# One weight tile moved off the bias table's buffers, and a load order changed, in a fused transformer layer

## The chip, the cores and the metric

The kernel runs on one core of one Trainium2 chip. The metric is the device time of one launch in microseconds; the median of three runs before the change is 919.48 us (918.82 to 919.53).

## The reference

One layer of a model with 512 tokens of width 1024, all in float32: a first gated feed-forward block (hidden width 2816), a mixer with two kinds of attention, a second feed-forward block, and a final norm. Cut to what matters here:

```python
def swiglu(x, w_gate, w_up, w_down):
    return (jax.nn.silu(x @ w_gate) * (x @ w_up)) @ w_down

x = x + 0.5 * swiglu(rmsnorm(x, ffn1_norm), ffn1_w_gate, ffn1_w_up, ffn1_w_down)
x = x + token_mixer(rmsnorm(x, mix_norm), w_in, w_out, ..., rel_bias)
x = x + 0.5 * swiglu(rmsnorm(x, ffn2_norm), ffn2_w_gate, ffn2_w_up, ffn2_w_down)
return rmsnorm(x, final_norm)
```

`rel_bias` (32 buckets by 16 heads) is spread into one row of biases per head before the mixer's attention starts. The change touches the end of the first feed-forward block, where `... @ w_down` is formed and the bias rows are made in passing.

## The kernel before

**Precision.** Every float32 matrix is split into a high part (a cast, on ACT) and a low part (the rest, a subtraction on DVE). A product is three matmuls into the same PSUM bank (lines 174, 175 and 176 of a helper): high by high, high by low, low by high. Where a weight block is the moving operand, the first and third matmul read its high part and the second (line 175) its low part. So each 128x512 weight block costs a load, a cast on ACT (line 469), a subtraction on DVE (line 473) and matmuls on PE.

**The down projection of the first block.** The 22 hidden tiles of 128 fall into 2 "plain" ones (`PLAIN`, tiles 0 and 1) and two groups of ten. Each group is five pairs of tiles, and is computed with seven block products instead of eight (Strassen's scheme): `a11`, `a22`, `s2`, `a12`, `s1`, `s3`, `s4`, in that order, each over the five pairs (index 0 to 4). One step (`STEP`, 1410 in the planner's units of about a nanosecond) is one pair of one product. In the second group the product of the plain tiles for the first half of the tokens, 24 matmuls into the banks `pc`, stands between `s1` and `s3`; its other half follows after the group.

**What feeds them.** The left upper weight blocks for `a11` are loaded into tiles `ra` (`raa` in the traces; pairs 0 and 1, and 2 and 3, share one 128x1024 buffer each, pair 4 has one of its own), those for `a22` into `re` (`place` puts pair 0 into the tile `rbc_n`, pairs 1 and 2 into two `ob` tiles `rea`, pair 3 into `sq`, pair 4 into a slot, also named `rea`). Sums of blocks (`sCa` for `s1`, `sBa` for `s3`) are loaded by SP and added to by a second, accumulating DMA from POOL. The blocks of `a12` are `rba`, `rbc_n` and `sq` again.

**What sets the order.** On all engines the order of instructions in this stage is the program's own. A planner puts events with times on a heap and emits them in order of time; each engine then runs its part in that order and waits only on semaphores. The table `TURNED["a"]` holds the numbers. Its entry `ahead` says for each product how many steps before the start of its *group* the load of each pair is emitted (`block_events`, with `block_load` doing the load). SP issues nearly all plain loads, and a load whose buffer is not free yet holds up those behind it.

**The plain weights.** At the group's end the weights of the two plain tiles come as four 128x512 blocks: output columns 0 to 511 (`dh` 0) and 512 to 1023 (`dh` 1), two blocks each. `plain_load` loads them, `plain_high` casts the high part (line 1254), `plain_low` subtracts for the low part (line 1257), each between the casts and subtractions of the products `s2` and `a12`. For `dh` 0 high and low part lie in the first two thirds of the tile `wx`, a buffer of 128x3072 with the tag `tx`. For `dh` 1 they are two tiles `wxh` and `wxl` of 128x1280 with the tag `pr1`. That tag has two buffers, which its tiles take in turn: a new tile waits until everything that used the tile two before it is done.

**The bias table.** `bias_load` takes a tile `ac` of the same tag `pr1` for the table (16x640). ACT and DVE change it in place (`bias_rows`, lines 1224 and 1228), and POOL stores it to DRAM as `bias_rows` (line 1229). The attention reads it back from there in strips (line 1234).

Of the kernel before, what the change touches and what calls it, by code (L numbers as in the profile page):

```python
# [15 lines left out]
F32R = mybir.dt.float32r  # L16
# [5 lines left out]
P = 128  # L22
# [54 lines left out]
    "b": {"plain": 2, "pairs": ((2, 4, 6, 8, 10), (12, 14, 16, 18, 20)),  # L77
          "sets": {2: (2, 3, 24, 25, 20, 21, 26), 4: (28, 29, 30, 31, 32, 33, 34), 6: (35, 36, 37, 38, 39, 40, 41),
# [23 lines left out]
HS = S // 2  # L102
# [11 lines left out]
def tile_macaron(ctx: ExitStack, tc, xs, xT, wf, wgu1, wst1, wdg1, wqk, wvw, wv, wo, wgu2, wst2,  # L114
# [7 lines left out]
    tp = ctx.enter_context(tc.tile_pool(name="tp", bufs=2))  # L122
# [1130 lines left out]
    def cast(o, a):  # L1253
        A.copy(o, a)
# [4 lines left out]
    closing, early_w, early_raw = {}, {}, {}  # L1259
# [9 lines left out]
    def plain_high(dh, k):  # L1269
        if k == 0:  # L1270
            if dh == 0:
                tx = tp.tile([P, 12 * HS], F32R, tag="tx", name="wx", bufs=1)
                closing[dh] = tx[:, :1024], tx[:, 1024:2048]
            else:
                closing[dh] = [tp.tile([P, 5 * HS], F32R, tag="pr1", name=f"wx{n}")[:, :1024] for n in "hl"]
        cast(closing[dh][0][:, k * 512:(k + 1) * 512], closing["raw", dh][k])

    def plain_low(dh, k):
# [66 lines left out]
    def close(at, begin, end, ah, al):  # L1345
        closing["tiles"] = ah, al
        gap = begin + 25 * STEP
        last = gap + TILES_STEP + 5 * STEP
        todo = [(begin + 2 * STEP, 1.5, plain_load, 0), (begin + 3 * STEP, 1.5, plain_load, 1),
                (begin + 5 * STEP, 1.5, early_load, 0, 0), (begin + 7 * STEP, 1.5, early_load, 0, 1),  # L1350
                (begin + 20.5 * STEP, 5, A.activation, root[:], eps[:], AF.Sqrt),
                (last - 1.8 * STEP, 1.6, early_load, 1, 0),
                (last + 0.4 * STEP, 1.6, early_load, 1, 1)]
        for n, t in enumerate((10, 11.5, 13, 14.5)):
            todo.append((begin + t * STEP, 4.5, plain_high, n // 2, n % 2))
            todo.append((begin + (t + 1) * STEP, 2.6, plain_low, n // 2, n % 2))
        for t, part in ((-4.2, (0, 0, 0, 512)), (-3.4, (0, 0, 512, 512)), (-2.6, (0, 1, 0, 512)), (-1.8, (0, 1, 512, 512))):
            todo.append((gap + t * STEP, 4.6, early_high, *part))
            todo.append((gap + (t + 0.9) * STEP, 2.7, early_low, *part))
        for tt in range(2):  # L1360
            t = gap + (tt + 1) * TILES_STEP // 2
            for dh in range(2):
                todo.append((t - (1 - dh) * TILES_STEP // 4 + 100, 0, plain_add, dh, tt))
            todo.append((t + 0.6 * STEP, 4, squared, 0, tt))
        for tt in range(2):
            todo += [(last + (0.6 + 0.5 * tt) * STEP, 4, squared, 1, tt),
                     (last + (1.3 + 0.8 * tt) * STEP, 0, mean, tt),
                     (last + (1.6 + 0.8 * tt) * STEP, 0, root_part, tt)]
            todo += [(last + (2.0 + 0.8 * tt) * STEP, 3, scaled, dh, tt) for dh in range(2)]
        for time, rank, f, *a in todo:  # L1370
            at(time, rank, f, *a)
        return plain_mm
# [869 lines left out]
```

## Time and profile before

| | |
|---|---|
| median of 3 runs | 919.48 us (918.82 to 919.53) |
| profiled execution, its own time | 921.12 us |
| its span, first to last instruction | 919.3 us |
| PE / DVE / ACT / POOL busy | 908.2 / 733.0 / 558.3 / 98.8 us |
| mean granted TensorE clock | 0.997 |
| first block's second group: `a11` starts | 280.32 us into the span |
| plain product starts | 320.12 us into the span |

Busy times are sums over one execution. PE is busy nearly throughout, so what can be gained is where it isn't, or where its matmuls follow each other more slowly than elsewhere. Times in the timeline are counted from the start of the span. A figure in square brackets is the time for which the engine sat idle before the instruction, with what ended the wait by the profile's inference. Where a wait is for several things, the profile names the one that it takes to be last; if the named one was done long before, it was another.

### The profile page before, as it was taken

How to read it: one execution, taken by the hardware profiler on the slowest of the kernel's cores; microseconds unless marked ns; L12 is line 12 of the kernel's file. 1: busy time of each engine (PE TensorE's matmuls, PEld its weight loads, DVE VectorE, ACT ScalarE, POOL GpSimd, SP SyncE). 2: the span in 40 equal slices, each digit the busy share in tenths (PEclk: the TensorE clock that was granted, in tenths of full speed). 3: DMA queues.
4: the chain of work that ended last, by engine and by line, in shares of the span. 5: the costliest groups of instructions: out<-in, count | busy, mean ns of one | idle time of the engine just before them, and what ended most of it. 6: DMA issues, size and time to landing. Idle time of an engine off the chain costs nothing.

```text
span 919.3 us, 16048 instructions
## 1 busy us (share of the span) xinstructions
PE 908.2 (99%) x5778; PEld 819.0 (89%) x5778; DVE 733.0 (80%) x1531; ACT 558.3 (61%) x1185; POOL 98.8 (11%) x123
## 2 busy tenths in 40 slices
PE   9999999999999899999999999999999999999997
PEld 7888998899998689888988878989999889999885
DVE  7798998878888687757866536798888887888886
ACT  7445765465667446655776676657665536666664
POOL 0001102121211000000000000010211213112200
PEclk9999999999999999999999999999999999999999
DMA  7454878587878513324434204355878859778722
GB/s 260 123 152 133 228 218 229 115 206 213 201 189 251 160 47 98 92 93 115 138 107 123 69 24 138 92 149 134 207 171 250 192 134 251 178 188 202 219 80 91
DMA packets 67247, 143.88 MB, mean 157 GB/s; under 512 B 7712, under 2 KB 8224, under 8 KB 67168
## 3 DMA queue, kind: packets, MB, share of 16 engines
q1 hardware_dynamic: 51312, 113.81, 38.1%
q0 software_dynamic: 15856, 29.06, 19.6%
q8 instruction: 45, 0.74, 0.3%
q14 instruction: 34, 0.28, 0.1%
HBM read 137.55 MB, written 2.14 MB: 152 GB/s over the span
## 4 chain that ended last, share of the span: by engine, by line
PE 91%; DVE 4%; DMA 3%; ACT 1%; issue 1%; SPq 0%; DVEq 0%; ACTq 0%
PE pt L175 6%; PE pt L174 6%; PE pt L176 6%; PE pq L174 2%; PE pwo L174 2%; PE pq L175 2%; PE pq L176 2%; PE pk L174 2%; PE pk L176 2%; PE pk L175 2%; PE pwo L175 2%; PE pwo L176 2%; PE pua L174 2%; PE pua L176 2%; PE pua L175 2%; PE pga L174 1%
## 5 line engine op out<-in xcount | busy, mean ns | idle before, releaser
L1735 ACT ACTIVATE pr<-pr,mx 128x128 f32<-128x128 f32 (+3 forms) x64 | 36.0, 563 | 36.7 <-DVE mx L1732 36.4
L569 DVE SCALAR_TENSOR_TENSOR x<-pt,x 128x512 f32<-128x512 f32 x52 | 34.4, 686 | 19.4 <-PE pt L176 14.0
L1732 DVE CUSTOM_DVE_ANT_0 pr<-sc,strip 128x128 f32<-128x128 f32 (+3 forms) x64 | 30.5, 489 | 23.1 <-PE sc L1730 22.6
L405 POOL DMA_DIRECT2D s1bg<-wst_dram x10 | 8.7, 868 | 333.4 <-DVE fin L1391 233.3
L473 DVE TENSOR_TENSOR w<-s2b,w 128x512 fp32r<-128x512 f32 x38 | 26.1, 686 | 7.0 <-ACT w L469 7.0
L469 ACT CAST w<-raa 128x512 fp32r<-128x512 f32 x31 | 19.0, 621 | 18.7 <-DVE raa L432 8.0
L469 ACT CAST w<-s2b 128x512 fp32r<-128x512 f32 x38 | 23.6, 620 | 8.4 <-DVE s2b L437 8.4
L174 PE MATMUL pwo<-w,mh 128*128 128x512 f32 x64 | 25.9, 404 | 0.0
L175 PE MATMUL pwo<-w,mh 128*128 128x512 f32 x64 | 25.0, 391 | 0.0
L176 PE MATMUL pwo<-w,ml 128*128 128x512 f32 x64 | 25.0, 391 | 0.0
L473 DVE TENSOR_TENSOR w<-s2a,w 128x512 fp32r<-128x512 f32 x30 | 20.5, 685 | 4.4 <-ACT w L469 4.3
L1523 DVE TENSOR_TENSOR w<-raw_qk,w 128x512 fp32r<-128x512 f32 x24 | 16.4, 687 | 7.9 <-ACT w L1519 7.8
L469 ACT CAST w<-s2a 128x512 fp32r<-128x512 f32 x30 | 18.6, 621 | 6.4 <-DVE s2a L437 6.0
L175 PE MATMUL pxgb<-ttb,w 128*128 128x256 f32 x80 | 22.5, 281 | 0.0
L469 ACT CAST w<-rab 128x512 fp32r<-128x512 f32 x26 | 15.7, 621 | 9.6 <-PE pt L176 5.6
L473 DVE TENSOR_TENSOR w<-raa,w 128x512 fp32r<-128x512 f32 x31 | 20.7, 680 | 0.0
L405 POOL DMA_DIRECT2D s1ag<-wst_dram x8 | 7.1, 888 | 125.0 <-DVE ala L275 40.1
L1729 PE MATMUL sc<-k,q 128*128 128x128 f32 (+3 forms) x64 | 20.5, 322 | 0.0
L1730 PE MATMUL sc<-l,q 128*128 128x128 f32 (+3 forms) x64 | 20.2, 322 | 0.0
L175 PE MATMUL pxub<-ttb,w 128*128 128x256 f32 x72 | 20.2, 281 | 0.0
L175 PE MATMUL pwga<-xl,w 128*128 128x256 f32 x64 | 18.0, 281 | 0.0
L176 PE MATMUL pwga<-xh,w 128*128 128x256 f32 x64 | 18.0, 281 | 0.0
(1101 smaller groups left out, 3921.9 us busy)
## 6 DMA issues: line engine op xcount, KB each, us to landing
raw_qk<-wqk_dram SPq DMA_DIRECT2D x12, 512.0 KB, 3.5
raw0bg<-wst_dram SPq DMA_DIRECT2D x10, 512.0 KB, 4.8
raw0bu<-wst_dram SPq DMA_DIRECT2D x9, 512.0 KB, 5.8
raw_gua<-wgu_dram SPq DMA_DIRECT2D x8, 512.0 KB, 3.6
raw0ag<-wst_dram SPq DMA_DIRECT2D x8, 512.0 KB, 5.0
strip<-bias_rows SPq DMA_DIRECT2D x16, 256.0 KB, 3.5
raw_wo<-wo_dram SPq DMA_DIRECT2D x8, 512.0 KB, 3.4
raw0au<-wst_dram SPq DMA_DIRECT2D x7, 512.0 KB, 6.7
```

The source lines that it names most:

```text
L174: T.matmul(po, wh, mh, start=first, stop=False, skip_group_check=on)
L175: T.matmul(po, wh, ml, start=False, stop=False, skip_group_check=on)
L176: T.matmul(po, wl, mh, start=False, stop=last, skip_group_check=on)
L405: nc.gpsimd.dma_start(t[:], b, accum_op=ALU.add)
L469: A.copy(made[t][0], source(t))
L473: V.tensor_tensor(l, source(t), h.bitcast(F32), op=ALU.subtract)
L569: V.scalar_tensor_tensor(o, a, f, b, op0=ALU.mult, op1=op1)
L1523: V.tensor_tensor(l[:, c:c + 512], raw[:, c:c + 512], h[:, c:c + 512].bitcast(F32), op=ALU.subtract)
L1729: T.matmul(ps[:, :w], qs[:, qi], ks[:, :w], start=True, stop=False)
L1730: T.matmul(ps[:, :w], qs[:, qi], ls[:, :w], start=False, stop=True)
L1732: V.tensor_tensor_reduce(out=pi, in0=ps[:, :w], in1=st["b"][m][:, w - 1::-1], op0=ALU.add, op1=ALU.min, scale=1.0, scalar=3.0e38, accum_ou ...
L1735: A.activation(pi, pi, AF.Exp, scale=-1.0, bias=st["mx"][:, m, i:i + 1], accum_out=st["ls"][:, m, i:i + 1])
```

## The change

Two edits, no other:

```diff
-                    "a11": ((11, 10, 5.9, 5.8, 4.6), (11, 10, 5.9, 5.8, 6)),
-                    "a22": ((6.5, 6.3, 3.8, 0.5, 5), (6.5, 6.3, 3.8, 0.5, 4)),
+                    "a11": ((11, 10, 5.9, 5.8, 4.6), (11, 10, 5.9, 5.8, 4.8)),
+                    "a22": ((4.4, 4.2, 3.2, 0.5, 1.5),) * 2,
...
             if dh == 0:
-                tx = tp.tile([P, 12 * HS], F32R, tag="tx", name="wx", bufs=1)
+                tx = closing["tx"] = tp.tile([P, 12 * HS], F32R, tag="tx", name="wx", bufs=1)
                 closing[dh] = tx[:, :1024], tx[:, 1024:2048]
             else:
-                closing[dh] = [tp.tile([P, 5 * HS], F32R, tag="pr1", name=f"wx{n}")[:, :1024] for n in "hl"]
+                closing[dh] = (closing["tx"][:, 2048:],
+                               tp.tile([P, 5 * HS], F32R, tag="pr1", name="wxl")[:, :1024])
```

**The tiles.** The high part of the plain weights with `dh` 1 goes into the last third of `wx`, which was unused. Only the low part `wxl` still takes a `pr1` buffer. Before, `wxh` took the buffer that follows the bias table's and `wxl` the bias table's own; now `wxl` takes the one that `wxh` had. No instruction moves by this. What changes is what an instruction waits for. DVE at the two low parts of `dh` 1, before, with the semaphores that each row waits for (`DMASW` are those of the DMAs from POOL, `DMAHW` those of the DMAs from SP):

```order
L473 TENSOR_TENSOR w<-rba_3308,w 128x512 [waits DMAHW0_49,Activation_49]
L1257 TENSOR_TENSOR wxl<-deadh_3274,wxh 128x512 [waits DMAHW3_49,DMASW3_49,Activation_49]
L569 SCALAR_TENSOR_TENSOR x_100<-pt_3221,x_100 128x512 [waits Activation_49]
L569 SCALAR_TENSOR_TENSOR x_101<-pt_3222,x_101 128x512 [waits Activation_49]
L473 TENSOR_TENSOR w<-sq,w 128x512 [waits DMAHW3_49,PE_49]
L1257 TENSOR_TENSOR wxl<-deadl_3275,wxh 128x512 [waits DMAHW4_49]
```

And after:

```order
L473 TENSOR_TENSOR w<-rba_3308,w 128x512 [waits DMAHW0_49,Activation_49]
L1257 TENSOR_TENSOR wxl<-deadh_3274,wx 128x512 [waits DMAHW3_49,Activation_49]
L569 SCALAR_TENSOR_TENSOR x_100<-pt_3221,x_100 128x512 [waits Activation_49]
L569 SCALAR_TENSOR_TENSOR x_101<-pt_3222,x_101 128x512 [waits Activation_49]
L473 TENSOR_TENSOR w<-sq,w 128x512 [waits DMAHW3_49,PE_49]
L1257 TENSOR_TENSOR wxl<-deadl_3275,wx 128x512 [waits DMAHW4_49]
```

The rows are the same in the same order; the wait on `DMASW3` at the first row of line 1257 is gone.

**The loads.** On SP, the loads for `a22` move behind those for `a11` in both groups of the first block. SP at the start of the second group, before (`raa` are blocks of `a11`; `rbc_n`, `rea` and `sq` of `a22`; `sBa` of `s3`):

```order
L516 DMA rbc_n_401<-wdg_dram 128x512
L516 DMA rea_3111<-wdg_dram 128x512
L505 DMA raa_3115<-wdg_dram 128x512
L510 DMA raa_3131<-wdg_dram 128x512 x2
L516 DMA rea_3150<-wdg_dram 128x512
L516 DMA rea_3166<-wdg_dram 128x512
L516 DMA sq<-wdg_dram 128x512
L523 DMA sBa_3248<-wdg_dram 128x512
```

And after:

```order
L510 DMA raa_3126<-wdg_dram 128x512 x2
L505 DMA raa_3144<-wdg_dram 128x512
L516 DMA rbc_n_401<-wdg_dram 128x512
L516 DMA rea_3147<-wdg_dram 128x512
L516 DMA rea_3164<-wdg_dram 128x512
L516 DMA rea_3195<-wdg_dram 128x512
L516 DMA sq<-wdg_dram 128x512
L523 DMA sBa_3248<-wdg_dram 128x512
```

The three later loads of `a11` have passed the first two of `a22`. In the first group the same happens around the loads of residual tiles `x` that stand between. PE, DVE, ACT and POOL keep their order in the whole program.

## The prediction

> **What bounds the kernel now.** I read the page first, for which engine the time hangs on:
>
> ```profile
> span 919.3 us, 16048 instructions
> PE 908.2 (99%) x5778; PEld 819.0 (89%) x5778; DVE 733.0 (80%) x1531; ACT 558.3 (61%) x1185; POOL 98.8 (11%) x123
> PE 91%; DVE 4%; DMA 3%; ACT 1%; issue 1%; SPq 0%; DVEq 0%; ACTq 0%
> ```
>
> PE is busy for 908.2 of 919.3 us, and the chain that ended last runs on PE for 91%. The change neither removes nor adds a matmul, so it can only act where PE stands still or runs slowly. The list of waits of PE alone says where it stands still after its warm-up:
>
> ```profile
> PE pt L175 <- DVE w L473: 3.3, 2, 3.1
> PE pt L1820 <- ACT ptx L1822: 0.2, 1, 0.2
> ```
>
> One gap of 3.1 us, a small one behind it in the same two lines (0.2), and nothing else longer than 0.2. PE's timeline at the long one, in the product `a12` of the second group:
>
> ```profile
> 301.52 0.39 PE L174 MATMUL pt<-w,h1a 128*128 128x512 f32 x1
> ...
> 305.60 0.39 PE L174 MATMUL pt<-w,h1a 128*128 128x512 f32 x1
> 309.05 0.50 PE L175 MATMUL pt<-w,h1a 128*128 128x512 f32 x1 [3.06 <-DVE w L473]
> 309.38 0.39 PE L176 MATMUL pt<-w,h2a 128*128 128x512 f32 x1
> ...
> 310.31 0.59 PE L174 MATMUL pt<-w,xl 128*128 128x512 f32 x1
> ...
> 313.69 0.43 PE L176 MATMUL pt<-w,h4a 128*128 128x512 f32 x1
> ```
>
> 18 matmuls start between 301.52 and 305.60, one each 0.227 us: the undisturbed pace. The next start comes 3.45 us later, at a matmul of line 175, which reads a low part. From 310.31 to 313.69 there are 8 starts, one each 0.42 us. The window over them shows why:
>
> ```profile
> 310.30:313.70 3.40, 3.40 (x10) 2.60 (x9) 2.93 (x6) 3.12 (x6) 0.00 (x0) 0.51 0.50 120
> ```
>
> The third column from the end is PE's granted clock: 0.51 for 3.4 us, about the ratio of 0.227 to 0.42. PE's idleness is paid a second time.
>
> What PE waited for is DVE's low part of a weight. DVE's own timeline:
>
> ```profile
> 299.84 1.27 DVE L473 TENSOR_TENSOR w<-rba,w 128x512 fp32r<-128x512 f32 x2
> 306.50 0.69 DVE L1257 TENSOR_TENSOR wxl<-deadh,wxh 128x512 fp32r<-128x512 f32 x1 [5.39 <-ACT w L469]
> 307.12 1.28 DVE L569 SCALAR_TENSOR_TENSOR x<-pt,x 128x512 f32<-128x512 f32 x2
> 308.31 0.68 DVE L473 TENSOR_TENSOR w<-sq,w 128x512 fp32r<-128x512 f32 x1
> ```
>
> DVE stood 5.39 us before `wxl`, with the low part that PE needed (`w<-sq`) three instructions behind it. The profile's releaser is a guess. Asked by tile, the store of the bias table says more:
>
> ```profile
> L1229 POOL DMA_DIRECT2D bias_rows<-ac x1: 762/762/762, 301.4 to 301.4; - x1
> DMA to landing us min/median/max: 5.0/5.0/5.0
> ```
>
> 301.4 + 5.0 = 306.4, and `wxl` starts at 306.50. `wxl` lies in the buffer from which that store reads, and waited for it to land.
>
> **Edit one: the tiles.** It takes that wait away: `wxl` goes where `wxh` was, and nothing on ACT had to wait for that buffer. The new place of `wxh` is the unused third of a tile already in use here. So DVE can start `wxl` at 301.1 (299.84 + 1.27). What is late next? Behind `wxl` stand two additions to `x`, which wait for ACT, and then `w<-sq`. By tile and on ACT:
>
> ```profile
> L513 SPq DMA_DIRECT2D sq<-wdg_dram x1: 327/327/327, 293.9 to 293.9; - x1
> DMA to landing us min/median/max: 7.8/7.8/7.8
> ...
> 301.79 0.62 ACT L469 CAST w<-sq 128x512 fp32r<-128x512 f32 x1 [2.61 <-PE pt L176]
> ...
> 302.83 1.06 ACT L557 COPY pt<-pt 128x512 f32<-128x512 f32 x2
> ```
>
> The block in `sq` lands at 293.9 + 7.8 = 301.7, so its cast starts at 301.79 and the two copies end at 302.83 + 1.06 = 303.89. The first addition can start after the first copy, at about 303.4, the second at 304.0, and `w<-sq` takes 304.6 to 305.3. PE wants it right after its matmul at 305.60, at 305.83. That leaves 0.5 us: PE doesn't stop, but this is next. If the additions wait for both copies, it is 0.1.
>
> The saving is thus: idle start to start 309.05 - 305.60 - 0.23 = 3.22; the slow restart 309.38 - 309.05 - 0.23 = 0.10; half clock 3.38 - 8 x 0.227 = 1.56. Sum 4.9 us. All of PE's later work moves forward by this, since its list holds no wait over 0.2 us behind it, and the loads there are released by engines that move too.
>
> The Trainium skill (TensorE: Matmul & The Clock Gate, Part 1) says that the clock falls to half after at least one idle window of about 3.4 us, windows that run freely. The trace agrees on the half and on the 3.4 us for which it lasts, but 3.06 us idle sufficed; what the rule would change is a rival below.
>
> **Edit two: the loads.** The small gap is at the start of the same group, where pair 2 of `a11` comes late:
>
> ```profile
> 271.64 0.68 DVE L439 TENSOR_TENSOR s2a<-raw0au,s2a 128x512 f32<-128x512 f32 x1
> 271.27 0.33 SPq L516 DMA_DIRECT2D rbc_n<-wdg_dram  x1
> 272.45 0.37 SPq L505 DMA_DIRECT2D raa<-wdg_dram  x1
> 272.92 0.89 SPq L510 DMA_DIRECT2D raa<-wdg_dram  x2
> DMA to landing us min/median/max: 7.8/7.9/8.1
> 280.88 0.62 ACT L469 CAST w<-raa 128x512 fp32r<-128x512 f32 x1 [4.07 <-DMA raa<-wdg_dram]
> 283.09 0.39 PE L174 MATMUL pt<-w,h0a 128*128 128x512 f32 x1
> 283.72 0.50 PE L175 MATMUL pt<-w,h0a 128*128 128x512 f32 x1 [0.24 <-DVE w L473]
> 284.05 0.39 PE L176 MATMUL pt<-w,h0a 128*128 128x512 f32 x1
> ```
>
> (The landing row is that of the three `raa` loads here.) Three loads stand ahead of it. ACT waits 4.07 us for it, and PE loses 283.72 - 283.09 - 0.23 = 0.40 and 284.05 - 283.72 - 0.23 = 0.10, together 0.5 us. After the change pair 2 goes first, as soon as its buffer's last reader on DVE is done at 271.64 + 0.68 = 272.3, with nothing new ahead of it. Between 272.3 + 2.5 (a quiet queue: `rbc_n` here takes 2.6) and 272.3 + 7.9 it lands between 274.8 and 280.2. I take about 276, nearer the quiet end, since the load in its new place is the one that was quick: the 0.5 us go. At the other end 0.6 us of its delay go, more than the 0.5 that it cost, so the same. A gain over 0.5 is excluded here, since PE loses no more.
>
> By the Trainium skill (DMA: Bandwidth & Descriptors, Anatomy of one DMA), a fit for loads from GpSimd, 256 KB would take an estimated 2.6 us; were that so here, pair 2 would have landed by 275.5, the second edit would be worth nothing and the time 0.5 us higher. The row of 7.9 us decides against it.
>
> What the moved loads of `a22` lose is cover. `rbc_n` now follows at about 273.7 (272.3, and three issues of 0.45):
>
> ```profile
> 283.28 0.62 ACT L469 CAST w<-rbc_n 128x512 fp32r<-128x512 f32 x1
> 140.12 0.39 PE L174 MATMUL pt<-w,h5a 128*128 128x512 f32 x1
> 124.98 0.33 SPq L516 DMA_DIRECT2D rbc_n<-wdg_dram  x1
> 126.58 0.80 SPq L510 DMA_DIRECT2D raa<-wdg_dram  x2
> ```
>
> With the longest landing of these rows, 8.1, it lands at 281.8, before the cast at 283.28: free. In the first group the same loads go from 124.98 to about 128.3 (126.58 and four issues), and would land by 136.4; `a22` starts on PE at 140.12 there, and its first block must have landed 1.3 us ahead (cast 0.62, subtraction 0.68). PE has no wait there before, so nothing is gained either.
>
> A debit: with PE 0.5 us earlier, `w<-sq` is wanted at 305.33, while its load may land no earlier, ready at 305.3 (or 305.7 in the worse case): 0 to 0.4 us, I take 0.1, near the case in which the copies release the additions one by one.
>
> **The sum.** 4.9 + 0.5 - 0.1 = 5.3 us, made against the profiled execution's own time of 921.12 (its span and 1.82 around it): 915.8. The median of the runs is 1.64 lower, 919.48; less 5.3 it is **914.2**. Bounds of this case: 5.4 and 4.5 off, with 0.5 for the runs' own spread (919.53 - 918.82 = 0.7): 913.6 to 915.5.
>
> **Rivals.**
>
> *The timed runs had no half clock.* The profiled execution is 1.64 us above the median, and the half-clock stretch costs 1.56. Its gap of 3.2 us is just shorter than the 3.4 us stretch; whether a gap trips the clock may differ between runs. Then only 3.22 + 0.10 + 0.4 = 3.7 us go: 915.8. For it speaks that near-equality; against it that profiling can itself cost something, and that the three runs lie within 0.7, where a gate that trips by chance would spread them by 1.6. The Trainium skill's rule of an idle window (TensorE: Matmul & The Clock Gate, Part 1), taken literally, gives this case. 20%.
>
> *The next wait takes over.* If the load into `sq` lands later than 302.2 in the timed runs, each further microsecond is one of PE. For it: the queue there is long (7.8 us to landing). Against: nothing in SP's order changes near it. A microsecond or two: 915.2 to 916.2, more only with the half clock again, 917.7. 8%.
>
> *Slower: the loads of `a22` come too late.* In the second group `a22` would start 30 matmuls behind the group's 280.32, at 287.1, and its first low part is wanted at 287.3, so the block must have landed by 286.0. To come out slower by 0.2%, the two groups must lose 5.3 + 1.8 = 7.1 us, 3.6 each: 2.0 idle and 1.6 of half clock. Then `rbc_n` lands at 288, 14.3 us after its issue; it begins to hurt at 12.3. The longest in the rows is 8.1. At 16 us each way: 919.48 - 5.3 + 2 x (3.7 + 1.6) = 924.8. 5%.
>
> *The wait stays.* If another user of the new buffer holds `wxl` (before, it was a tile read by PE's gate and up products, which end where the group starts at 280.32): 919.0 with the second edit alone. 3%.
>
> **How the numbers follow.** The main case has 64%. About 0.2%, 1.8 us, is what a measurement of this kernel can tell from no change, so faster means below 917.6. Main case, half-clock rival and most of the takeover are faster: 0.64 + 0.20 + 0.06 = 0.90. Same: the wait stays, the rest of the takeover: 0.05. Slower: 0.05. The range goes from 913.2 to 916.6: the main case, the half-clock rival with its own spread, and most of the takeover.
>
> **What would show it.** In the profile of the changed kernel: no idle time at line 1257 before `wxl`; no wait of PE over 0.3 us in the second group; granted clock 1.00 between 303 and 316; the plain product starting near 315 instead of 320.12; pair 2 of `a11` cast before 280. Wrong would be: DVE still standing at `wxl`; PE waiting at `w<-rbc_n` or `w<-rea`; a wait of PE further back that eats what was won; or a span that shrinks by 5 while the timed median shrinks by 3 to 4 (the half-clock rival).

## The result, and the profile after

The changed kernel takes 915.47 us (median of 6 runs, 914.77 to 917.04) against 919.46 us before (6 runs, 917.83 to 919.53): a ratio of 0.9964, with a 95% interval of 0.9951 to 0.9977, so it is 4.0 us faster. The forecast was 5.3. Its profiled execution is the longest of the six, 917.04 us with a span of 915.2. Three lines of its page:

```profile
span 915.2 us, 16047 instructions
PE 906.7 (99%) x5778; PEld 818.9 (89%) x5778; DVE 733.0 (80%) x1531; ACT 558.6 (61%) x1185; POOL 98.7 (11%) x123
PE 96%; DVE 2%; ACT 1%; DMA 0%; issue 0%; DVEq 0%; SPq 0%; ACTq 0%
```

The chain that ended last runs on PE for 96% now, and the DMAs have left it. All waits of PE in the changed kernel:

```profile
PE warm L1149 <- POOL ones_d L1143: 1.0, 1, 1.0
PE pga L1194 <- ACT w L1174: 0.9, 1, 0.9
PE pt L1821 <- ACT ptx L1823: 0.2, 1, 0.2
```

The first two are the start of the kernel, the third stands in the attention. Both gaps of the second group are gone. DVE's timeline there, after:

```profile
299.93 1.27 DVE L473 TENSOR_TENSOR w<-rba,w 128x512 fp32r<-128x512 f32 x2
301.13 0.67 DVE L1257 TENSOR_TENSOR wxl<-deadh,wx 128x512 fp32r<-128x512 f32 x1
303.75 1.29 DVE L569 SCALAR_TENSOR_TENSOR x<-pt,x 128x512 f32<-128x512 f32 x2 [1.95 <-ACT pt L557]
304.96 0.68 DVE L473 TENSOR_TENSOR w<-sq,w 128x512 fp32r<-128x512 f32 x1
```

`wxl` follows the subtractions at once, where it stood for 5.39 us. DVE now waits 1.95 us for ACT's copies, one step further on, and PE doesn't feel it. The windows around the old gap, after (busy time and count of each engine, then PE's granted clock, the DMA share and GB/s):

```profile
303.00:310.00 7.00, 7.00 (x33) 5.79 (x32) 6.07 (x10) 5.73 (x10) 0.88 (x1) 1.00 0.64 115
310.00:316.00 6.00, 6.00 (x28) 4.99 (x27) 4.18 (x8) 3.96 (x9) 0.00 (x0) 1.00 0.77 239
316.00:320.00 4.00, 4.00 (x20) 3.30 (x19) 3.86 (x8) 1.61 (x4) 0.00 (x0) 1.00 0.00 0
```

The clock is at 1.00 throughout, and PE has 33, 28 and 20 matmuls in the three, where the same windows of before have 18, 21 and 19.

**Two starts that differ.** The span fell by 4.1 us only, and the group starts later than before, at 282.06 instead of 280.32. That comes from the kernel's first 30 us, which the change doesn't touch. The window from 7 to 10 us, before:

```profile
7.00:10.00 3.00, 3.00 (x15) 2.46 (x14) 2.30 (x4) 3.00 (x7) 0.00 (x0) 1.00 1.03 371
```

and after:

```profile
7.00:10.00 3.00, 3.00 (x9) 2.29 (x8) 2.55 (x5) 3.00 (x6) 0.00 (x0) 1.00 1.01 376
```

A little later on PE's timeline, a matmul that both kernels have, before:

```profile
28.45 0.49 PE L174 MATMUL pga<-eha,w 128*128 128x512 f32 x1
```

and after:

```profile
30.17 0.49 PE L174 MATMUL pga<-eha,w 128*128 128x512 f32 x1
```

Two things are in this. The first of these matmuls itself starts 0.62 us later, as it waits longer for ACT's cast. Before:

```profile
5.02 0.79 PE L1194 MATMUL pga<-eha,w 128*128 128x512 f32 x1 [0.24 <-ACT w L1174]
```

and after:

```profile
5.64 0.79 PE L1194 MATMUL pga<-eha,w 128*128 128x512 f32 x1 [0.86 <-ACT w L1174]
```

The other 1.1 us are pace: between 7 and 10 us PE did 15 matmuls before and 9 after, though the granted clock reads 1.00 in both, so PE reached its full pace later. From the matmul of line 174 to the end the two spans are 919.3 - 28.45 = 890.85 and 915.2 - 30.17 = 885.03: 5.8 us less, while the start took 1.72 away. In nine of the ten profiles that follow, of kernels with and without the change, that matmul stands between 27.90 and 28.26, in the tenth at 28.84. So this profile of the changed kernel had a slow start by chance, and that of the kernel before, as will be seen, a long gap by chance.

### The profile page after: what moved, and what is told of

Its sections match the earlier page's. It is cut to its first block, busy times and chain, and to the rows that moved or that the text cites. A ratio compares the mean times of both kernels' runs of the same rounds, so it can differ in the third digit from the quotient of the medians.

```text
span 915.2 us, 16047 instructions
## 1 busy us (share of the span) xinstructions
PE 906.7 (99%) x5778; PEld 818.9 (89%) x5778; DVE 733.0 (80%) x1531; ACT 558.6 (61%) x1185; POOL 98.7 (11%) x123
## 4 chain that ended last, share of the span: by engine, by line
PE 96%; DVE 2%; ACT 1%; DMA 0%; issue 0%; DVEq 0%; SPq 0%; ACTq 0%
PE pt L176 6%; PE pt L175 6%; PE pt L174 6%; PE pq L174 2%; PE pwo L174 2%; PE pq L176 2%; PE pk L174 2%; PE pq L175 2%; PE pk L176 2%; PE pk L175 2%; PE pwo L176 2%; PE pwo L175 2%; PE pua L174 2%; PE pua L176 2%; PE pua L175 2%; PE pga L174 1%
```

## Experiments

The theory: `wxl` waited for the store of the bias table, the move of its tile takes that wait away, and the loads give half a microsecond more. The rival is that the half clock behind the gap is in some executions only. Against both stands that the gain comes from elsewhere, from the load order for instance.

**The two edits apart.** `before_again` is the kernel before, unchanged, and `after_again` the changed one; all four ran on one chip beside 23 runs of the kernel before (median 918.59). The tiles alone:

```diff
-                tx = tp.tile([P, 12 * HS], F32R, tag="tx", name="wx", bufs=1)
+                tx = closing["tx"] = tp.tile([P, 12 * HS], F32R, tag="tx", name="wx", bufs=1)
...
-                closing[dh] = [tp.tile([P, 5 * HS], F32R, tag="pr1", name=f"wx{n}")[:, :1024] for n in "hl"]
+                closing[dh] = (closing["tx"][:, 2048:],
+                               tp.tile([P, 5 * HS], F32R, tag="pr1", name="wxl")[:, :1024])
```

The loads alone:

```diff
-                    "a11": ((11, 10, 5.9, 5.8, 4.6), (11, 10, 5.9, 5.8, 6)),
-                    "a22": ((6.5, 6.3, 3.8, 0.5, 5), (6.5, 6.3, 3.8, 0.5, 4)),
+                    "a11": ((11, 10, 5.9, 5.8, 4.6), (11, 10, 5.9, 5.8, 4.8)),
+                    "a22": ((4.4, 4.2, 3.2, 0.5, 1.5),) * 2,
```

The kernel before, again:

> The kernel before, unchanged, as an experiment: how its runs scatter and whether its gap of 3.1 us at the bias table's store is followed by half clock in every run. Theory 1 (half clock in every run; the shortfall of 1.3 us against the forecast of 5.3 is the luck of the start-up): mean granted clock 0.997 or less in nearly all runs, and the new profile shows 0.5 for 3.4 us behind the gap again. Theory 2 (the gap trips the clock only now and then): clock of 0.998 or 0.999 in most runs, times in two heaps about 1.6 us apart, and the new profile more likely than not without the stretch. Either way ratio 1.000 within 0.002.

The changed kernel, again:

> The changed kernel, unchanged: no gap and no half clock behind the start in any run, so what scatters here is the start-up alone. Theory 1: 5 us under the kernel before on this chip, 914 to 915. Theory 2: 3.7 to 4.2 us under it, as in the result. Both: start-up later or earlier by up to 1.7 us in the profile, PE without a wait over 0.2 us between 10 us and the end.

The tiles alone:

> Only the tiles of the plain weights moved, the loads as before. My theory: the wait before wxl goes and with it PE's long gap, 4.9 us with half clock behind it in the run before, 3.3 without; the gap of 0.4 to 0.5 us at the second group's start stays. So 0.5 us slower than both edits. Rival (the loads carry the gain): time as before.

The loads alone:

> Only the loads of the first block's second products moved, the tiles as before. My theory: the small gap at the second group's start goes (0.5 us), the wait before wxl stays with its 5.4 us on DVE and 3.1 us on PE; as the store of the bias table hangs on PE's progress and on loads, PE's gap may grow by the 0.5 us won, so 0 to 0.5 us faster than before. Rival (moved loads come too late): PE waits at w<-rbc_n or w<-rea, slower than before.

Measured:

| kernel | runs | median us (range) | ratio to before [95%] |
|---|---|---|---|
| before, again | 12 | 918.87 (917.17 to 921.49) | 0.9998 [0.9985, 1.0011] |
| both edits | 5 | 915.02 (914.69 to 915.35) | 0.9952 [0.9934, 0.9970] |
| tiles alone | 5 | 915.11 (914.51 to 915.65) | 0.9953 [0.9937, 0.9970] |
| loads alone | 12 | 917.74 (916.98 to 921.04) | 0.9994 [0.9982, 1.0006] |

The tiles carry the whole measurable gain, 918.59 - 915.11 = 3.5 us; both edits give 3.6. The loads alone can't be told from no change.

The profile of `before_again` (own time 917.49) looks different from the one that the prediction was built on. On DVE's timeline:

```profile
304.63 0.69 DVE L1257 TENSOR_TENSOR wxl<-deadh,wxh 128x512 fp32r<-128x512 f32 x1 [5.45 <-ACT w L469]
```

on PE's:

```profile
307.18 0.50 PE L175 MATMUL pt<-w,h1a 128*128 128x512 f32 x1 [2.25 <-DVE w L473]
```

and in the window behind PE's gap:

```profile
307.20:310.60 3.40, 3.40 (x15) 2.83 (x16) 3.40 (x6) 1.90 (x2) 0.00 (x0) 1.00 0.43 89
```

DVE waits as long, but PE's gap is 2.25 us instead of 3.06, and behind it the clock stays at 1.00: 15 matmuls in 3.4 us, where there were 10. There is no loss at the start of the group either. Its span of 915.7 is 2.5 us above the 913.2 of `after_again`, which is its gap (2.25 idle, 0.16 more from start to start, 0.10 for the slow restart).

Why the gap has another size shows on POOL. The kernel before, in its first profile:

```profile
300.76 0.86 POOL L524 DMA_DIRECT2D sBa<-wdg_dram  x1 [2.16 <-PE pt L175]
301.38 0.76 POOL L1229 DMA_DIRECT2D bias_rows<-ac  x1
```

and in `before_again`:

```profile
297.40 0.86 POOL L524 DMA_DIRECT2D sBa<-wdg_dram  x1 [0.86 <-PE pt L176]
298.01 0.76 POOL L1229 DMA_DIRECT2D bias_rows<-ac  x1
```

with, asked by tile, the time to landing of `bias_rows` in `before_again` (the longest is the store's, the other two are strips):

```profile
DMA to landing us min/median/max: 3.2/3.3/6.5
```

The store stands behind an accumulating load of `s3` in POOL's order. That load was let go at 300.76 in one execution and at 297.40 in the other, and the store took 5.0 and 6.5 us to land.

What let it go later can be followed back in the traces. It adds to a block that a plain load of SP brings, here the fourth into `sBa`. In all six profiles with the old tiles, four of which come below, it goes 0.8 to 0.9 us after that plain load has landed. In the table, the second and third column are counted from the start of the group; the third is SP's load into `rbc_n` for `a12`, which stands ahead of the plain load on SP:

| profile | pair 2 of `a11` cast | `rbc_n` loaded | plain load issued + landing | accumulating load goes |
|---|---|---|---|---|
| before | +0.56 | +6.91 | 291.43 + 8.5 = 299.9 | 300.76 |
| store early | +0.14 | +6.49 | 291.13 + 7.3 = 298.4 | 299.36 |
| before, again | -1.06 | +5.29 | 289.58 + 7.0 = 296.6 | 297.40 |
| before, a third profile | -1.17 | +5.25 | 290.01 + 7.6 = 297.6 | 298.52 |
| store late | -1.74 | +5.25 | 289.86 + 8.9 = 298.8 | 299.61 |
| loads alone | -2.76 | +5.24 | 289.61 + 8.1 = 297.7 | 298.62 |

Of the 3.36 us between the first two profiles of the kernel before, 1.85 are a later issue of the plain load and 1.5 a longer landing. The later issue goes with the late pair 2 of `a11`: with the cast a microsecond or more ahead of the group's start, the load into `rbc_n` comes 5.24 to 5.29 us behind that start, and with a later cast at 6.49 and 6.91. SP waits there for DVE's last subtraction from that tile, on DVE's and SP's timelines of the first profile:

```profile
286.52 0.68 DVE L473 TENSOR_TENSOR w<-rbc_n,w 128x512 fp32r<-128x512 f32 x1
287.23 0.33 SPq L513 DMA_DIRECT2D rbc_n<-wdg_dram  x1
```

So the late block, which the prediction priced at 0.5 us, also delayed the store in that profile, by an estimated 1.7 us (6.91 less 5.25). How much of PE's gap this makes was not measured apart, and the landing of the plain load (7.0 to 8.9 us) scatters as much by itself.

In `tiles_only` the wait that the prediction named as next can be seen. ACT's timeline:

```profile
301.26 0.62 ACT L469 CAST w<-sq 128x512 fp32r<-128x512 f32 x1 [2.09 <-DMA sq<-wdg_dram]
```

DVE's:

```profile
302.91 1.29 DVE L569 SCALAR_TENSOR_TENSOR x<-pt,x 128x512 f32<-128x512 f32 x2 [2.94 <-ACT pt L557]
304.12 0.68 DVE L473 TENSOR_TENSOR w<-sq,w 128x512 fp32r<-128x512 f32 x1
```

and PE's:

```profile
304.32 0.39 PE L174 MATMUL pt<-w,h1a 128*128 128x512 f32 x1
304.86 0.50 PE L175 MATMUL pt<-w,h1a 128*128 128x512 f32 x1
```

The load into `sq` landed 8.4 us after its issue, and PE's start is 304.86 - 304.32 - 0.23 = 0.31 late, with 0.10 behind it. In `after_again` the same two starts are 0.23 apart.

**The store moved, the tiles left alone.** If the store sets the gap, then moving it in the kernel before must move the gap. The four steps of `bias_rows` are placed by one line; the last holds the store, and with it a few small instructions of ACT and one of DVE on the table. Each one product step earlier (`store_early`), which puts the store ahead of that accumulating load:

```diff
-                    at(starts[begin["t", 1] + 2 + j], 5, bias[1], j)
+                    at(starts[begin["t", 1] + 1 + j], 5, bias[1], j)
```

The last step six product steps later (`store_late`), behind the last accumulating load:

```diff
-                    at(starts[begin["t", 1] + 2 + j], 5, bias[1], j)
+                    at(starts[begin["t", 1] + 2 + j + 6 * (j == 3)], 5, bias[1], j)
```

Of the early one was expected:

> The kernel before, with the four steps that make and store the bias table one planner step earlier; tiles and loads untouched. On POOL the store stands ahead of the fourth accumulating load of s3 instead of behind it. My theory (DVE waits at wxl for the store's landing): store issued near 296.5 to 298.6 us, landed 5 us later, so DVE stands 0.5 to 2.5 us at wxl instead of 5.4, PE's gap shrinks from 2.3 to 3.1 us to 0.5 or less, no half clock behind it; time within 0.5 of the tiles alone, 915 to 916. Rival (wxl waits for something else, ACT's cast as the profile names it): gap and time as before.

and of the late one:

> The kernel before, with the last step of the bias table (its store with it) six planner steps later, so that POOL stores behind the last accumulating load of s3. My theory: the store lands 4 to 6 us later, PE's gap grows to 6 to 8 us, and now the clock falls to half behind it in every run: 922 to 925, clock 0.997 or less in all. Rival (half clock is the luck of the run, whatever the gap): clock 0.999 in half of the runs, two heaps as before. Rival for the cause (wxl doesn't wait for the store): time as before.

`store_early` took 916.07 us (12 runs, 915.02 to 917.59), ratio 0.9972 [0.9961, 0.9984]; `store_late` 924.27 (6 runs, 923.22 to 925.30), ratio 1.0061 [1.0040, 1.0082], beside 17 runs of the kernel before on their chip (median 918.44). In the profile of `store_early`, on the timelines of POOL, DVE and PE:

```profile
297.39 0.76 POOL L1229 DMA_DIRECT2D bias_rows<-ac  x1
```

```profile
303.92 0.69 DVE L1257 TENSOR_TENSOR wxl<-deadh,wxh 128x512 fp32r<-128x512 f32 x1 [3.64 <-ACT w L469]
```

```profile
306.47 0.50 PE L175 MATMUL pt<-w,h1a 128*128 128x512 f32 x1 [1.35 <-DVE w L473]
```

The gap shrank to 1.35 us and not to the 0.5 or less that was expected, because the store still took 6.4 us to land (297.4 to 303.8); the time came out just above the 915 to 916 expected. The theory holds, the estimate of the landing didn't. In that of `store_late`, on the timelines of DVE and PE, and in the window around the gap's end:

```profile
308.77 0.69 DVE L1257 TENSOR_TENSOR wxl<-deadh,wxh 128x512 fp32r<-128x512 f32 x1 [8.92 <-DMA bias_rows<-ac]
```

```profile
311.32 0.80 PE L175 MATMUL pt<-w,h1a 128*128 128x512 f32 x1 [5.70 <-DVE w L473]
```

```profile
310.95:314.36 3.41, 3.04 (x7) 2.46 (x8) 3.32 (x6) 0.46 (x1) 0.00 (x0) 0.50 0.04 15
```

Here the profile itself names the store's DMA as what ended DVE's wait, since everything else was long done. The gap is 5.7 us, a little under the 6 to 8 expected, and the clock is at half for 3.41 us, from shortly before its end. The stores' landings and DVE's starts over all of these kernels:

| profile | store issued + landing | `wxl` starts | PE idle | half clock |
|---|---|---|---|---|
| store early | 297.4 + 6.4 = 303.8 | 303.92 | 1.35 | no |
| loads alone | 299.2 + 5.2 = 304.4 | 304.48 | 2.09 | no |
| before, again | 298.0 + 6.5 = 304.5 | 304.63 | 2.25 | no |
| before, a third profile | 299.1 + 5.6 = 304.7 | 304.84 | 2.33 | no |
| before | 301.4 + 5.0 = 306.4 | 306.50 | 3.06 | yes |
| store late | 305.0 + 3.5 = 308.5 | 308.77 | 5.70 | yes |

`wxl` starts 0.1 to 0.3 us behind the landing in all six. The cast that it reads was done long before, between 297.8 and 299.2 in the six; on ACT's timeline in the first profile:

```profile
298.56 0.61 ACT L1254 CAST wxh<-deadh 128x512 fp32r<-128x512 f32 x1
```

That the wait for the store is the cause is thus shown both ways, by the tile taken away from it and by the store moved.

**How often the half clock comes.** A run without a trace still has its mean granted clock: 0.997 in the two profiles with the stretch, 0.998 or 0.999 in the profiles of the kernels before and after that have none. The kernel before ran 52 times in these two comparisons:

| mean clock | runs | median us | range |
|---|---|---|---|
| 0.997 or less | 23 | 919.64 | 918.81 to 921.72 |
| 0.998 or more | 29 | 917.52 | 916.82 to 918.70 |

None of the 22 runs of `after_again`, `tiles_only` and `store_early` has 0.997 or less, all six of `store_late` have, and of `loads_only`, where `wxl` waits as before, 3 of 12. The line between the two isn't quite sharp: one more run of `loads_only` (919.37 us) and one of the kernel before on the chip of the last experiment (919.99) have 0.998 at times like those of the upper row. So the half clock comes in an estimated 23 of 52 executions of the kernel before, by the clock and not by a trace of each. The two heaps of times lie 2.1 us apart, 1.6 of which is the half clock; the rest may be longer gaps in the runs that trip (those in which the clock falls). Whether the clock falls by chance at equal gaps, or whenever the gap passes some size between the 2.33 us that left it alone and the 3.06 us that didn't, these runs don't show. Five of the six runs of `store_late` have a mean clock of 0.995 or 0.996, where its profile, with one stretch of 3.41 us, has 0.997: by this estimate they spent longer at half.

**How much cover the later loads of `a22` have.** In the changed kernel, with four of the five in each group later by another 5 to 6 steps:

```diff
-                    "a22": ((4.4, 4.2, 3.2, 0.5, 1.5),) * 2,
+                    "a22": ((-0.9, -1.9, -2.9, 0.5, -4.5),) * 2,
```

> The changed kernel with the loads of the second products moved much further back: the first behind that into sq, the second and third behind loads that wait for PE and DVE, the last far back. It shows what the slower rival would cost. Theory (the cover of the changed kernel is ample, but what is late hurts in full): the third block is issued only when the first is used up, lands 3 to 4 us after it is wanted in each group, and PE waits there: 4 to 10 us over the changed kernel, half clock included. Rival (loads of these products never bind): 915.

It took 931.99 us (4 runs, 926.01 to 934.52), ratio 1.0134 [1.0099, 1.0169], 17 us above the changed kernel and far beyond what was expected. From PE's list of waits:

```profile
PE pt L174 <- ACT w L469: 9.8, 4, 4.3
```

the longest of the first and of the second group, on PE's timeline:

```profile
152.46 0.80 PE L174 MATMUL pt<-w,h5a 128*128 128x512 f32 x1 [3.93 <-ACT w L469]
...
304.44 0.51 PE L174 MATMUL pt<-w,h5a 128*128 128x512 f32 x1 [4.28 <-ACT w L469]
```

and the windows at them:

```profile
151.88:158.70 6.82, 6.24 (x14) 4.66 (x15) 6.26 (x11) 4.33 (x8) 2.18 (x3) 0.50 0.99 238
305.47:308.89 3.42, 3.42 (x9) 2.65 (x8) 2.72 (x6) 2.27 (x7) 0.86 (x1) 0.50 1.08 307
```

9.8 us of waits, and half clock for 6.82 and 3.42 us, in which PE was busy for 6.24 and 3.42; half of that is lost, 4.8: together 15 of the 18 us by which this execution (933.15) lies above that of `after_again`. The expectation had the stalls, but too few of them and the half clock too short. The way of coming out slower that the prediction named is thus real, and the change keeps clear of it: its profiles show no wait at these blocks.

**Three kernels once more,** on another chip, for the second edit's term: does pair 2 of `a11` cost PE anything when it lands late?

> The kernel before once more, for one more profile. Open is how often pair 2 of a11 comes late at the second group's start: PE lost 0.5 us there in the first profile and nothing in the second. Theory (the landing scatters with the queue, 6.4 to 7.9 us so far, and binds only above about 7): a loss between 0 and 0.7 us, and PE's long gap again 2 to 3.5 us. Rival (the first profile was a stray): no loss here.

> The tiles alone once more. Theory: pair 2 of a11 lands 5 to 8 us after its issue, as it did in the kernel before, and PE loses 0 to 0.7 us at the second group's start; at w<-sq PE may lose up to 0.5 us again (0.41 in the profile of the first such run). Rival: neither loss shows, then the loads' edit has nothing to win.

> The changed kernel once more. Theory: pair 2 lands within 3 to 6 us, no loss at the second group's start; at w<-sq PE loses at most 0.4 us, as the load into sq lands late relative to PE. Rival: a loss at the group's start as without the loads' edit.

The kernel before took 917.81 us (span 916.0), the tiles alone 914.91 (913.1), both 914.80 (913.0), one run each. The cast of pair 2 on ACT's timeline in this profile of the kernel before:

```profile
278.96 0.62 ACT L469 CAST w<-raa 128x512 fp32r<-128x512 f32 x1 [2.34 <-PE pxua L176]
```

and in that at the changed one:

```profile
277.05 0.62 ACT L469 CAST w<-raa 128x512 fp32r<-128x512 f32 x1 [0.76 <-PE pyua L175]
```

Pair 2 is cast 1.9 us earlier in the changed kernel, and PE loses nothing at this place in any of the three: the group's first matmul starts at 280.13 and 279.81, and ACT was early enough in both. Of the seven profiles with the old load order, the first one lost 0.5 us at pair 2 and 0.15 at pair 3 behind it, `store_early` 0.25 at the two (its cast came at 280.04), and the other five nothing.

## Why the prediction was right, and where its terms were off

**The wait of `wxl`: right.** DVE has no idle time there, in any of the five profiles of the changed kernel and of the tiles alone. The store, not the ACT cast that the profile named, held it; moving the store, with the tiles left alone, moved the gap between 1.35 and 5.70 us.

**The gap (3.22 us from start to start): mis-sized for the median run.** The profile that it came from was one of the longer executions, 921.12 us, where six of the 52 later runs were over 921. Other profiles of the kernel before, and the one with the loads alone, have gaps of 2.1 to 2.3 us idle, 2.25 to 2.5 from start to start. In the first profile the store was issued 3.4 us later than in `before_again`; the late pair 2, priced by itself in the sum, had a part in that, so that two of the sum's terms were not independent.

**The half clock (1.56 us): right where it is, wrong in how often.** It counted as if each run had it. On the two chips with a clock on record for each run 23 of 52 do, and 23/52 x 1.56 = 0.7. Subtracting a sum made against an execution of 921.12 from a median that lay 1.64 lower gave the median run more loss than it had. The near-equality of 1.64 and 1.56 was on the page, and was given 20% as the rival without half clock. The argument against it, that three runs within 0.7 us can't hold two heaps 1.6 apart, fails: a heap that holds nearly half of the runs fills three draws about once in ten. That may be what happened: the six runs of the kernel before in the first measurement have no clock on record, but five of them (918.82 to 919.53) lie within the times of the upper row of the table of clocks, and one (917.83) within those of the lower. By their times most of them had the half clock, so that its share can explain little of the 1.3 us that were missing there.

**The rival without half clock: half right.** Its sign was a span that shrinks by 5 while the median shrinks by 3 to 4. The median shrank by 4.0 and 3.6; of the span, 5.8 us went behind the start. It said that the timed runs have none; on the two chips just named they have it in part, and in the first measurement, by their times, mostly. So the sign came without its cause being shown there. For the second measurement the mixture gives: for the runs without, 917.52 - 915.05 = 2.5 (the second number is the median of the ten runs of `after_again` and `tiles_only`), for those with, 919.64 - 915.05 = 4.6, together 29/52 x 2.5 + 23/52 x 4.6 = 3.4, beside 3.6 measured. The Trainium skill (TensorE: Matmul & The Clock Gate, Part 1), by which half clock follows at least one idle window of 3.4 us whose phase is free, is contradicted on the length by the 3.06 us that sufficed. That an equal program trips in some runs and not in others fits its free phase, and as well gaps that differ from run to run; no run here shows the window itself.

**The loads (0.5 us): the step happens, the cost was a single draw.** Pair 2 lands sooner (2.9 to 4.4 us after its issue in three profiles of the changed kernel, 5.4 to 7.9 with the old order), and is cast with no wait for the DMA. But the loss that this removes is in two of seven profiles. With the old tiles a late pair 2 also delays the store; whether that is why fewer runs of `loads_only` trip (3 of 12 beside 23 of 52), so few runs can't say. By the timed runs the edit is worth 0.1 us with the tiles (915.11 to 915.02), within the spread, so it is not shown to be worth anything.

**The next wait (debit of 0.1): about right.** It showed as 0.4 us in one profile of `tiles_only`, as nothing in the other four with the edit.

**The plain product** starts at 316.11 in the profile of the changed kernel, where near 315 was said; less the 1.72 us of its slow start it is 314.4.

**The sum.** 3.6 to 4.0 measured against 5.3. In the second measurement, with 3.6, the gap gives some 0.8 less in the runs without half clock, the share of the clock 0.9 less on average, the loads 0.4 less; the runs that trip seem to have longer gaps, which would give part of it back. In the first, with 4.0, the same reading leaves the loads, a shorter gap, and two long runs among the six of the changed kernel (917.04 and 916.84), which put their median 0.4 above the 915.05 of the ten later runs; how much each gave isn't shown. 915.47 lies in the range, as does the 915.02 of the second measurement, but the first is only just within the main case's own bounds (913.6 to 915.5): the mechanism was right, and the range was wide enough for the terms that were off.

## What to carry to other kernels

A temporary that shares a rotating tag with a tile still being stored waits for that store to land, and an engine that executes in order then holds up everything queued behind; ask which DMA last read the buffer when the releaser that the profile names was long done. Before a sum is made from one profiled execution, see where its own time lies among the runs: a term that depends on chance, like a half-clock stretch or a late landing, is to be multiplied by how often it comes. A spread of three runs says little on that; the mean granted clock of a dozen does. And ask whether two terms of the sum have one cause, as the late block and, in part, the late store had here.

## What the runs showed that had not been expected

A gap of 2 to 3 us on PE halves its clock in some executions and not in others. None of 12 runs tripped at a gap of 1.35 us, 23 of 52 at gaps of about 2.3 to 3.1, six of six at 5.7 (sizes by one to three profiles each, counts by the mean clock). In the profiles the clock then stays at half for 3.4 us, or for 6.8 as in the first group of `a22_late`.

The time until PE runs at its full pace differs between executions: 15 or 9 matmuls in the same 3 us, at a granted clock that reads 1.00 both times, and the matmul of line 174 behind the start at 30.17 us or, in the profile of `after_again`, at 28.11. Of the changed kernel's six runs in the first measurement, 917.04 and 916.84 us stand beside four of 914.77 to 915.59; only the first of these has a trace, so for the second a slow start is a guess.

A store of 16x640 floats, 41 KB, took 5.0 to 6.5 us to land in five of these profiles, and 3.5 us in that of `store_late`, where it went later: by the windows over the flight the DMA engines were busy 0.79 and 0.81 of it in the kernel before (its first two profiles), and 0.52 in `store_late`. That the busier engines are the reason is likely, but was not tested.
